# Recurrent layer: rates and scans of the first three chunks placed on either side of the sixth convolution; attention's norm broadcast issued one filling step earlier

## The chip, the cores and the metric

One NeuronCore of one Trainium2 chip runs the whole program. The metric is the time of one execution in device microseconds (us). A core has five engines that run side by side, each with its own queue, strictly in the order of that queue: TensorE (PE, matrix products into PSUM banks, with its weight loads PEld), VectorE (DVE), ScalarE (ACT), GpSimd (POOL) and SyncE (SP, which here only issues DMAs). Engines meet through semaphores: an instruction starts when its queue has reached it and what it waits for is done.

## The reference

Two layers of an encoder over 512 positions of width 1024, in float32. The first layer mixes by stick-breaking attention, the second by a gated recurrence; each is followed by an MLP, and a norm ends it.

```python
for layer in range(DEPTH):                       # DEPTH = 2
    h = rms_norm(x, norm_mix[layer])
    y = stick_breaking_attention(h, ...) if layer % 2 == 0 else rglru_block(h, ...)
    x = x + y
    h = rms_norm(x, norm_mlp[layer])
    x = x + squared_relu_mlp(h, mlp_w1[layer], mlp_w2[layer])
return rms_norm(x, norm_final)

def rglru_block(h, ...):
    proj = h @ w_in
    gate = jax.nn.gelu(proj[..., :RG_WIDTH])
    xc = causal_depthwise_conv(proj[..., RG_WIDTH:], conv_w, conv_b)       # 4 taps
    r = sigmoid(blocks(xc) @ w_a + b_a);  i = sigmoid(blocks(xc) @ w_x + b_x)   # 16 blocks of 64
    log_a = -8.0 * r * softplus(-lam)
    a = exp(log_a);  mult = sqrt(-expm1(2.0 * log_a))
    hs = scan over positions of (a, mult * i * xc)       # h[t] = a[t] h[t-1] + b[t]
    return (hs * gate) @ w_o
```

In the attention, `z` is the score of a query and a key, scaled; the weight of a key is sigmoid(z) times the product of sigmoid(-z) over the keys between it and the query.

## The kernel before

Activations lie transposed, 128 features by 512 positions, as eight chunks numbered 0 to 7. A float32 product is made of three fast ones: each operand is split into a high half (a copy by ACT, `wh`, `bh`, `xgh`) and a low half (a subtraction by DVE, `wl`, `bl`, `xgl`), and TensorE adds high x high, high x low and low x high (lines 197 to 199). A dense product of one chunk is 24 such products of 128x512 from one slab of weights (512 KB), which SP loads into `raw`, ACT copies to `wh` (line 185) and DVE subtracts to `wl` (line 192). From the fourth convolution to the last gate the low half of a slab is instead made by POOL (line 188) and a DMA that adds (line 189).

TensorE's order is written out by hand. The other engines' queues are laid out by a planner, which goes by priorities and by `issue_after` edges ("not before that instruction in the queue"): the helper `after(...)` sets one.

**Attention, first 105 us.** TensorE is filled with steps of dense products (queries, keys, values), and scores and values are slipped between them by due times. The norm of the input is not yet known when the first queries and keys are made; `inverse()` supplies it in two steps: after filling step `SUMS` = 5 the sums of squares are turned into `rc` and a diagonal `diag`, and after filling step `BROAD` = 9 a product with `diag` (line 422) broadcasts it over partitions and ACT copies it to SBUF as `r` (line 425). For the first pair of heads each score `z` is multiplied by `r` on DVE (`keep`, line 536) before ACT's two sigmoids (lines 538, 539) and DVE's scan (line 549). Scores turn through two `z` banks, so the third score waits until the first has been read by line 536.

**Recurrence, about 595 to 705 us.** The program's order is the list of calls at the end of `with ExitStack() as rctx`: `conv`, `gates`, `gate`, `recur`, `gated`. For chunk c,

- `conv(c)`: a dense product; DVE scales it by the norm (line 1071); ACT begins the convolution (1078) and DVE adds three taps (1080); ACT and DVE split it into high half (1086) and low half (1087). Convolutions have the planner's high priority.
- `gates(c)`: six products (lines 1100 to 1102, three for each of two gates; 1100 needs the high half, 1102 the low half), two sigmoids (1107, 1108), and `i * xc` on DVE (1109).
- `recur(chunks)`: for each chunk tanh (1119) and exp (1121) on ACT, 1122 and 1124 on DVE, 1123 on POOL; then for each chunk a square root (1127), a product (1128) and the scan (1131) on DVE.
- `gate(c)`: a dense product, scaled by the norm (1137). `gated(chunks)`: gelu (1142), product with the scan (1144), split (1145, 1146).

ACT changes its function table when it passes between sigmoid or tanh, exp, square root and gelu; each change is an instruction of its own, ACT_TABLE_LOAD. The chunks go through `recur` as 0 to 2, 3 to 5, and 6 and 7. The first group's call stands ahead of `conv(5)`, the sixth convolution. TensorE's order there is: convolution 4, gates 3, convolution 5, gates 4, gate 3, convolution 6, gates 5, gate 4, convolution 7, gates 6, gate 5, gate 6, gates 7, gate 7, then the output products.

Of the kernel before, what the change touches and what calls it, by code (L numbers as in the profile page):

```python
# [13 lines left out]
AF = mybir.ActivationFunctionType  # L14
ALU = mybir.AluOpType
# [5 lines left out]
C = D // P  # L21
# [19 lines left out]
HOLD = 3  # L41
LESS = 4
SUMS = 5
BROAD = 9
EARLY = 5


# [1 line left out]
def hybrid_encoder(  # L49
# [22 lines left out]
    V, A, G, PE = nc.vector, nc.scalar, nc.gpsimd, nc.tensor  # L72
# [941 lines left out]
    with ExitStack() as rctx:  # L1014
# [25 lines left out]
        def after(act):  # L1040

            return tc.issue_after(act.ins) if act is not None else nullcontext()

        xc, aa, om, z, hs, gin, gw = ({} for _ in range(7))

        TURNS = ["acc", "acc", "t", "t", "o", *("acc", "acc", "t", "t") * 3]
        turns = [0, 0]
# [44 lines left out]
        def gates(c):  # L1092
            nonlocal sig
            xch, xcl = gin[c]
            gh, gl = gw[c]
            pg = []
            for i in range(2):
                pi = bank("zzoo"[turns[1] % 4])
                turns[1] += 1
                PE.matmul(pi, gh[:, i, :], xch, start=True, stop=False)  # L1100
                PE.matmul(pi, gl[:, i, :], xch, start=False, stop=False)
                PE.matmul(pi, gh[:, i, :], xcl, start=False, stop=True)
                pg.append(pi)
            if c + 3 < C:
                gw[c + 3] = gate_weights(c + 3)
            with after(mark), after(begin):
                A.activation(aa[c], pg[0], AF.Sigmoid, bias=col("b_a")[:, c : c + 1])
                sig = A.activation(om[c], pg[1], AF.Sigmoid, bias=col("b_x")[:, c : c + 1])
            V.tensor_tensor(xc[c], om[c], xc[c], ALU.mult)

        def recur(chunks):
            nonlocal mark

            for c in chunks:
                a0 = rp2.tile([P, S], F32, tag="a0", name="a0")
                d = rp2.tile([P, S], F32, tag="d", name="d")

                with after(sig), after(high if c == 1 else None):
                    ex = A.activation(om[c], aa[c], AF.Tanh, scale=c4[:, c : c + 1])
                with after(ex):  # L1120
                    ex = A.activation(a0, aa[c], AF.Exp, scale=c8[:, c : c + 1])
                V.scalar_tensor_tensor(d, a0, 1.0, om[c], ALU.add, ALU.mult)
                G.tensor_scalar(aa[c], d, -1.0, 1.0, ALU.mult, ALU.add)
                V.scalar_tensor_tensor(xc[c], a0, 1.0, xc[c], ALU.add, ALU.mult)
            for c in chunks:
                with after(ex):
                    mark = A.activation(om[c], om[c], AF.Sqrt)
                V.tensor_tensor(xc[c], xc[c], om[c], ALU.mult)

                with after(tap if c < 6 else None):  # L1130
                    V.tensor_tensor_scan(om[c], aa[c], xc[c], 0.0, ALU.mult, ALU.add)
                hs[c] = om[c]

# [14 lines left out]
        sig = begin = tap = high = low = None  # L1148
        for what, c in (
            (conv, 0), (conv, 1), (conv, 2), (gate, 0), (gate, 1), (gates, 0), (conv, 3), (gates, 1),  # L1150
            (gate, 2), (gates, 2), (conv, 4), (gates, 3), (recur, range(3)), (conv, 5), (gates, 4),
            (gate, 3), (conv, 6), (gates, 5), (gate, 4), (conv, 7), (recur, range(3, 6)), (gates, 6),
            (gate, 5), (gated, range(6)), (gate, 6), (gates, 7), (recur, range(6, C)), (gate, 7),
            (gated, range(6, C)),
        ):
            with tc.high_priority() if what is conv else nullcontext():
                what(c)
# [166 lines left out]
```

## Time and profile before

| what | value |
|---|---|
| median of 3 runs | 1074.24 us (1074.09 to 1075.43) |
| the profiled execution's own time | 1074.38 us |
| its span, first to last instruction | 1072.4 us |
| TensorE busy | 1058.7 us, 99% |
| DVE / ACT / POOL busy | 821.3 / 568.6 / 170.8 us |
| granted TensorE clock | 0.998 |

The profiled execution takes 1.98 us more than its span and stands 0.14 us above the median. In the rows that follow, a timeline row gives start, duration, engine, line, operation, output and input, and in square brackets the idle time of the engine before it with what ended that time. A row of waits gives the total, the number of waits and the longest. "Busy" for TensorE is partly modelled, so short gaps between products are not seen as idle time.

### The profile page before, as it was taken

To read this page: it belongs to the slowest core of one execution; us is meant where nothing else is said; L and a number is where in the kernel's file an instruction comes from. 1 tells how busy PE (TensorE), PEld (TensorE's weight loads), DVE (VectorE), ACT (ScalarE), POOL (GpSimd) and SP (SyncE) were. 2 spreads that over 40 slices of the span, in tenths; PEclk is the share of its full clock that TensorE was granted. 3 is DMA by queue.
4 is the path that set the end of the run, shared out by engine and by line. 5 is a ranking of instruction groups with operands and counts; after the bars stand their busy time and mean duration, and the time that the engine had idled before them with its cause. 6 is when DMAs were issued, how large, how long until landed. Compare 5 with 4: busy or idle time off the path is not lost.

```text
span 1072.4 us, 13604 instructions
## 1 busy us (share of the span) xinstructions
PE 1058.7 (99%) x4992; PEld 878.4 (82%) x4992; DVE 821.3 (77%) x1073; ACT 568.6 (53%) x826; POOL 170.8 (16%) x199
## 2 busy tenths in 40 slices
PE   9999999999999999999999999999999999999997
PEld 7888888888888888888888877887888888888885
DVE  7788787839896697596688869975786597597777
ACT  6777676726554444344345477944454344344345
POOL 2344443410000000000001655122000000000003
PEclk9999999999999999999999999999999999999999
DMA  7745454517215206305342694243205305305103
GB/s 237 198 118 145 128 146 107 171 53 255 79 40 182 93 20 179 116 15 183 99 85 72 167 215 130 82 174 101 95 24 192 99 20 177 118 13 184 60 12 107
DMA packets 44034, 125.71 MB, mean 117 GB/s; under 512 B 7744, under 2 KB 8512, under 8 KB 43968
## 3 DMA queue, kind: packets, MB, share of 16 engines
q1 hardware_dynamic: 41088, 115.94, 34.7%
q0 software_dynamic: 2304, 8.39, 4.5%
q8 instruction: 39, 0.64, 0.3%
q10 hardware_dynamic: 576, 0.52, 0.2%
q14 instruction: 27, 0.22, 0.1%
HBM read 104.91 MB, written 2.10 MB: 100 GB/s over the span
## 4 chain that ended last, share of the span: by engine, by line
PE 88%; DVE 6%; ACT 3%; DMA 1%; issue 1%; SPq 0%; ACTq 0%; DVEq 0%
PE ps_t L874 9%; PE ps_acc L199 6%; PE ps_acc L197 6%; PE ps_acc L198 6%; PE ps_o L874 6%; PE ps_z L874 6%; PE ps_acc L874 4%; PE ps_o L197 4%; PE ps_o L198 4%; PE ps_o L199 4%; PE ps_t L198 4%; PE ps_t L197 3%; PE ps_t L199 3%; PE ps_z L198 3%; PE ps_z L197 3%; PE ps_z L199 3%
## 5 line engine op out<-in xcount | busy, mean ns | idle before, releaser
L185 ACT CAST wh<-raw 128x1024 fp32r<-128x1024 f32 (+2 forms) x136 | 119.7, 900 | 129.8 <-PE ps_o L199 33.6
L840 ACT CAST wh<-b 128x1024 fp32r<-128x1024 f32 x96 | 100.3, 1051 | 132.0 <-PE ps_o L874 25.0
L192 DVE TENSOR_TENSOR wl<-raw,wh 128x1024 fp32r<-128x1024 f32 (+2 forms) x126 | 131.0, 1056 | 23.3 <-ACT wh L185 23.1
L841 DVE TENSOR_TENSOR wl<-b,wh 128x1024 fp32r<-128x1024 f32 x96 | 118.4, 1236 | 23.9 <-ACT wh L840 23.8
L197 PE MATMUL ps_acc<-xgh,wh 128*128 128x512 f32 x304 | 122.5, 403 | 0.4 <-ACT wh L166 0.4
L199 PE MATMUL ps_acc<-xgl,wh 128*128 128x512 f32 x304 | 119.1, 392 | 0.1
L198 PE MATMUL ps_acc<-xgh,wl 128*128 128x512 f32 x304 | 119.0, 392 | 0.1
L855 POOL DMA_DIRECT2D b<-in_w_dn x6 | 5.4, 905 | 637.8 <-DVE wl L841 314.9
L549 DVE TENSOR_TENSOR_SCAN scan<-keep,later 128x128 f32<-128x128 f32 (+1 forms) x64 | 58.1, 911 | 17.4 <-ACT keep L539 10.6
L197 PE MATMUL ps_o<-xgh,wh 128*128 128x512 f32 x176 | 69.5, 395 | 0.2 <-DVE x L701 0.2
L198 PE MATMUL ps_o<-xgh,wl 128*128 128x512 f32 x176 | 68.6, 390 | 0.0
L199 PE MATMUL ps_o<-xgl,wh 128*128 128x512 f32 x176 | 68.6, 390 | 0.0
L199 PEld LDWEIGHTS ps_acc<-xgl,wh 128*128 128x128 f32 x304 | 57.1, 188 | 12.7 <-DVE xgl L117 0.5
L794 ACT ACTIVATE u<-u 128x512 f32<-128x512 f32 x64 | 39.3, 630 | 52.1 <-DVE u L793 52.1
L197 PE MATMUL ps_t<-xgh,wh 128*128 128x512 f32 x168 | 66.5, 396 | 0.0
L197 PEld LDWEIGHTS ps_acc<-xgh,wh 128*128 128x128 f32 x304 | 57.3, 188 | 10.6 <-ACT wh L166 0.7
L198 PE MATMUL ps_t<-xgh,wl 128*128 128x512 f32 x168 | 65.7, 391 | 0.0
L198 PEld LDWEIGHTS ps_acc<-xgh,wl 128*128 128x128 f32 x304 | 57.3, 188 | 10.1 <-DVE wl L167 0.8
L199 PE MATMUL ps_t<-xgl,wh 128*128 128x512 f32 x168 | 65.5, 390 | 0.0
L553 POOL TENSOR_TENSOR w<-w,scan 128x128 f32<-128x128 f32 (+1 forms) x64 | 51.9, 813 | 53.6 <-DVE scan L549 50.8
L862 DVE TENSOR_TENSOR b<-b,b 128x1024 f32<-128x1024 f32 x46 | 55.9, 1217 | 0.2
L804 DVE TENSOR_TENSOR u<-u 128x256 f32<-128x256 f32 x128 | 49.4, 419 | 2.4 <-ACT u L794 1.7
(325 smaller groups left out, 2749.1 us busy)
## 6 DMA issues: line engine op xcount, KB each, us to landing
raw<-in_w_m SPq DMA_DIRECT2D x64, 512.0 KB, 3.6
b<-in_w_dn SPq DMA_DIRECT2D x48, 512.0 KB, 4.2
raw<-in_w_dn SPq DMA_DIRECT2D x16, 512.0 KB, 3.5
raw<-in_w_in SPq DMA_DIRECT2D x16, 512.0 KB, 4.2
raw<-in_w_qk SPq DMA_DIRECT2D x12, 512.0 KB, 3.6
wl<-raw POOLq DMA_DIRECT2D x10, 512.0 KB, 6.2
x<-in_xT SPq DMA_DIRECT2D x16, 256.0 KB, 4.2
raw<-in_w_ro SPq DMA_DIRECT2D x8, 512.0 KB, 4.2
```

Source lines behind the costliest of these rows:

```text
L185: A.copy(wh[:, k, :], raw[:, k, :])
L192: V.tensor_tensor(wl[:, k, :], raw[:, k, :], f(wh[:, k, :]), ALU.subtract)
L197: PE.matmul(ps, wh, ah, start=start, stop=False)
L198: PE.matmul(ps, wl, ah, start=False, stop=False)
L199: PE.matmul(ps, wh, al, start=False, stop=stop)
L549: V.tensor_tensor_scan(sc[:, S - n : S][:, ::-1], keep[:, :n][:, ::-1], later[:, S - n :][:, ::-1], 1.0, ALU.mult, ALU.max,)
L553: G.tensor_tensor(wt, wt, sc[:, S - n + 1 : S + 1], ALU.mult)
L804: V.tensor_tensor(u[:, out, :], u[:, x, :], u[:, y, :], op)
L840: A.copy(wh, raw)
L841: self.cut = V.tensor_tensor(wl, raw, f(wh), ALU.subtract)
L862: self.sum = V.tensor_tensor(raw, raw, self.raws[to, g], ALU.add)
L874: PE.matmul(ps, x[:, block, ts], y[:, jj, cols], start=first and n == 0, stop=last and n == 2, skip_group_check=not new,)
```

## The change

Two things are changed.

First, `recur` is cut in two. `rates(chunks)` is its first half, tanh, exp and the three element operations; the new `recur(chunks)` is its second half, square root, product and scan. For the first group `rates` stays ahead of `conv(5)`, and `recur` is called behind it, with new edges: square roots not ahead of ACT's begin of convolution 5, products and scans not ahead of the low half of convolution 5 (`low`). For the other groups the two are called one behind the other. In the first group the edge to a high half (`high`) moves from the tanh of chunk 1 to the exp of chunk 0, so all three tanh go ahead of the split of convolution 4, and its exp behind it. In `gates`, `i * xc` (line 1109, now 1110) gets an edge behind the latest low half.

Second, `BROAD` goes from 9 to 8.

```diff
-BROAD = 9
+BROAD = 8
...
-            V.tensor_tensor(xc[c], om[c], xc[c], ALU.mult)
-
-        def recur(chunks):
-            nonlocal mark
+            with after(low):
+                V.tensor_tensor(xc[c], om[c], xc[c], ALU.mult)
+
+        def rates(chunks):
 
             for c in chunks:
                 a0 = rp2.tile([P, S], F32, tag="a0", name="a0")
                 d = rp2.tile([P, S], F32, tag="d", name="d")
-
-                with after(sig), after(high if c == 1 else None):
+                with after(sig):
                     ex = A.activation(om[c], aa[c], AF.Tanh, scale=c4[:, c : c + 1])
-                with after(ex):
+
+                with after(ex), after(high if c == 0 else None):
                     ex = A.activation(a0, aa[c], AF.Exp, scale=c8[:, c : c + 1])
...
+            exps[chunks[-1]] = ex
+
+        def recur(chunks):
+            nonlocal mark
             for c in chunks:
-                with after(ex):
+
+
+                with after(exps[chunks[-1]]), after(begin if c < 3 else None):
                     mark = A.activation(om[c], om[c], AF.Sqrt)
-                V.tensor_tensor(xc[c], xc[c], om[c], ALU.mult)
-
-                with after(tap if c < 6 else None):
+                with after(low if c < 3 else None):
+                    V.tensor_tensor(xc[c], xc[c], om[c], ALU.mult)
+                with after(low if c < 3 else tap if c < 6 else None):
                     V.tensor_tensor_scan(om[c], aa[c], xc[c], 0.0, ALU.mult, ALU.add)
...
-            (gate, 2), (gates, 2), (conv, 4), (gates, 3), (recur, range(3)), (conv, 5), (gates, 4),
-            (gate, 3), (conv, 6), (gates, 5), (gate, 4), (conv, 7), (recur, range(3, 6)), (gates, 6),
-            (gate, 5), (gated, range(6)), (gate, 6), (gates, 7), (recur, range(6, C)), (gate, 7),
+            (gate, 2), (gates, 2), (conv, 4), (gates, 3), (rates, range(3)), (conv, 5),
+            (recur, range(3)), (gates, 4),
+            (gate, 3), (conv, 6), (gates, 5), (gate, 4), (conv, 7), (rates, range(3, 6)), (recur, range(3, 6)), (gates, 6),
+            (gate, 5), (gated, range(6)), (gate, 6), (gates, 7), (rates, range(6, C)), (recur, range(6, C)), (gate, 7),
```

No instruction's shape or count changes and no arithmetic does. TensorE's order stays, but for the broadcast product, which goes ahead of one step (three products). On the other engines the order can be listed from the built programs without running them. In the recurrence, behind the edges named above: on DVE the three products 1128 and the three scans 1131 of the first group, which lay between the taps of convolution 5, stand together behind its low half and ahead of line 1071 of convolution 6; further on, the scaled gate 5 (1137) and the subtraction of a `w_ro` slab (192) stand ahead of the low half of convolution 7, not behind it; on ACT the split of convolution 6 stands ahead of the third tanh of the second group. In the attention: ACT's copy of `r` goes ahead of the split of the second pair's queries (line 312), DVE's first `keep` (536) stands behind two subtractions of line 192 that followed it, and ahead of the low half of those queries (313); a later slab of `w_qk` is loaded ahead of four copies of queries on SP's queue, copied by ACT between the first sigmoids, and subtracted by DVE around the third `keep`, where all three came later before.

More of the change, by code (lines that the diff above doesn't have):

```diff
@@ L1042, in after @@
             return tc.issue_after(act.ins) if act is not None else nullcontext()
-        xc, aa, om, z, hs, gin, gw = ({} for _ in range(7))
+        xc, aa, om, z, hs, gin, gw, exps = ({} for _ in range(8))
         TURNS = ["acc", "acc", "t", "t", "o", *("acc", "acc", "t", "t") * 3]
```

## The prediction

> **What bounds the kernel now.** I read the page first (its head and its first part), then TensorE's waits, then the timeline of each engine around the longest of them.
>
> ```profile
> span 1072.4 us, 13604 instructions
> PE 1058.7 (99%) x4992; PEld 878.4 (82%) x4992; DVE 821.3 (77%) x1073; ACT 568.6 (53%) x826; POOL 170.8 (16%) x199
> ```
>
> ```profile
> PE ps_o L1100 <- ACT bh L1086: 2.1, 1, 2.1
> PE ps_z L530 <- DVE keep L536: 1.2, 1, 1.2
> ...
> PE ps_z L1102 <- DVE bl L1087: 0.9, 2, 0.5
> ```
>
> TensorE is the bound: 13.7 us of the span are idle, most of it at the two ends. So time is won or lost only where TensorE waits, and the two longest waits inside are the two that the change stands beside. The most it can win is what these places cost, read from TensorE's timeline:
>
> ```profile
> 32.49 0.28 PE L448 MATMUL ps_acc<-wh,xgl 128*128 128x256 f32 x1
> 33.95 0.44 PE L530 MATMUL ps_z<-kh,q 128*128 128x384 f32 x1 [1.18 <-DVE keep L536]
> ...
> 640.54 0.39 PE L199 MATMUL ps_t<-xgl,wh 128*128 128x512 f32 x1
> 643.15 0.40 PE L1102 MATMUL ps_z<-bl,gh 128*128 128x512 f32 x1
> ...
> 654.22 0.39 PE L199 MATMUL ps_acc<-xgl,wh 128*128 128x512 f32 x1
> 656.68 0.50 PE L1100 MATMUL ps_o<-bh,gh 128*128 128x512 f32 x1 [2.07 <-ACT bh L1086]
> 658.21 0.39 PE L1102 MATMUL ps_o<-bl,gh 128*128 128x512 f32 x1
> 669.98 0.39 PE L1102 MATMUL ps_z<-bl,gh 128*128 128x512 f32 x1
> 682.30 0.39 PE L1102 MATMUL ps_o<-bl,gh 128*128 128x512 f32 x1
> ```
>
> Unhindered, 128x512 products start 0.23 us apart (rows of conv 4 and 5 stages; 0.23 x 6 = 1.4 for the six of a `gates`). Gates 4 should end with a start at 640.54 + 1.4 = 641.94 and do at 643.15: 1.2 lost. Gates 5: 655.6 against 658.21: 2.6 lost. With 0.2 of gates 2, the recurrence can give 4.0. The third score, due at 32.61, starts at 33.95: 1.34. Gates 6 and 7 (669.98 and 682.30 are their first products with a low half) wait for nothing now.
>
> **The attention part (`BROAD`).**
>
> ```profile
> 29.66 0.59 ACT L312 CAST xh<-ps_t 128x512 fp32r<-128x512 f32 x1 [4.63 <-DMA q<-xl]
> 30.14 0.59 ACT L425 COPY r<-ps_z 128x512 f32<-128x512 f32 x1
> ```
>
> ```profile
> 33.61 0.28 DVE L536 TENSOR_TENSOR keep<-ps_z,r 128x128 f32<-128x128 f32 x1
> ```
>
> ACT sits 4.63 us at line 312 until a DMA has read the buffer that it overwrites, and the copy of `r`, whose product was made long before, is queued behind it. Changed, the broadcast product goes one step (three products, 0.7 us) earlier, and `r` is queued ahead of line 312. Then `r`, two halves of a `w_v` slab and two of a `w_qk` slab are copied in the idle 4.63 us, DVE has four subtractions behind them (each 0.6, to 30.3), and the first `keep` ends near 30.6, not at 33.89. The third score finds its bank free at 32.61: **1.34 won**. Line 312 itself still starts at 29.66, so the second pair's queries are no sooner.
>
> Next behind it is the fifth score, now at 38.45, then due at 37.1, which waits for the third `keep`. Ahead of that `keep` DVE now has a subtraction of the next `w_qk` slab, whose copy blocks ACT until its load has landed. SP issues that load earlier, where its queue comes free of `kl`:
>
> ```profile
> 29.18 1.84 SPq L331 DMA_DIRECT2D kl<-tl  x2
> 34.34 0.58 SPq L179 DMA_DIRECT2D raw<-in_w_qk  x1
> ```
>
> ```profile
> DMA to landing us min/median/max: 3.8/3.8/3.8
> ...
> DMA to landing us min/median/max: 5.1/6.1/7.1
> ```
>
> The first row is this load at 34.34, the second the two `w_v` loads issued right behind it. Issued at 31.05 and landing L later, half a copy (0.62), half a subtraction (0.6), two hand-overs and the `keep` (0.54 for 128x384) follow: the `keep` ends at 32.9 + L. With L up to 4.2 the fifth score is in time; each microsecond more costs one. The bounds are 3.8 (nothing lost) and 7.1 (2.9 lost). I take 4.5, near the same load's own row, since four copies of `kl` and `kh` are still under way: 0.3 lost. The four query copies behind it on SP's queue are late by about 1 us; they serve scores of the second pair near 50 us, and cost nothing. Gain here: **1.05** (1.34 down to -1.6). The rest of attention is full TensorE time, and ACT and DVE there wait for scores, so the gain is carried on.
>
> **The recurrence: the waits removed.**
>
> ```profile
> 634.13 1.05 ACT L185 CAST wh<-raw 128x1024 fp32r<-128x1024 f32 x1 [3.05 <-PE ps_t L199]
> 637.21 0.72 ACT L1119 ACTIVATE om<-aa,c 128x512 f32<-128x512 f32 x1
> ...
> 640.47 0.60 ACT L1086 CAST bh<-bt 128x512 fp32r<-128x512 f32 x1
> ...
> 650.31 1.04 ACT L185 CAST wh<-raw 128x1024 fp32r<-128x1024 f32 x1
> 656.01 0.62 ACT L1086 CAST bh<-bt 128x512 fp32r<-128x512 f32 x1 [4.66 <-DVE bt L1080]
> 658.00 0.78 ACT L1078 ACTIVATE bt<-ps_acc,colt 128x512 f32<-128x512 f32 x1 [0.41 <-DVE ps_acc L1071]
> ...
> 661.84 0.72 ACT L1121 ACTIVATE a<-aa,c 128x512 f32<-128x512 f32 x1
> ```
>
> Changed, the high half of chunk 4 follows three tanh (0.63 each) on ACT, at 637.2 + 1.9 = 639.1 and not 640.47; its low half is done by 640.5, gates 4 (due 640.77, low 641.2) don't wait: 1.2 won. Between 634.13 and 651.35 ACT is never idle and does the same list of work in both orders (no table load more or less), so the high half of chunk 5 can start at 651.3 (651.1 with the 0.2 of gates 2). It started at 656.01 because DVE's last tap was behind two scans; with the scans behind the low half, the taps are done by 649, even with the third one held behind the scaled gate 3 (TensorE's end, 647.7). Low half of chunk 5 at 651.7 to 652.4; gates 5, due near 653 by then, don't wait: 2.6 won.
>
> **The recurrence: what is late next.** The scans don't vanish. Behind that low half DVE has three products, 1109 of chunk 4 and three scans, and only then line 1071 of convolution 6.
>
> ```profile
> 647.52 1.22 DVE L1131 TENSOR_TENSOR_SCAN om<-aa,bt 128x512 f32<-128x512 f32 x1
> 651.52 2.05 DVE L1131 TENSOR_TENSOR_SCAN om<-aa,bt 128x512 f32<-128x512 f32 x1
> 657.27 0.69 DVE L1071 TENSOR_TENSOR ps_acc<-ps_acc,r 128x512 f32<-128x512 f32 x1
> 665.07 0.68 DVE L1124 SCALAR_TENSOR_TENSOR bt<-a,bt 128x512 f32<-128x512 f32 x1
> 665.67 0.68 DVE L1137 TENSOR_TENSOR z<-ps_t,r 128x512 f32<-128x512 f32 x1
> 672.75 1.52 DVE L1080 SCALAR_TENSOR_TENSOR bt<-ps_t,colt,bt 128x511 f32<-128x511 f32 x2
> 676.41 3.44 DVE L1131 TENSOR_TENSOR_SCAN om<-aa,bt 128x512 f32<-128x512 f32 x3
> 679.77 0.66 DVE L1087 TENSOR_TENSOR bl<-bt,bh 128x512 fp32r<-128x512 f32 x1
> 683.97 1.21 DVE L192 TENSOR_TENSOR wl<-raw,wh 128x1024 fp32r<-128x1024 f32 x1
> ...
> 701.87 1.29 DVE L1146 TENSOR_TENSOR bl<-z,bh 128x512 fp32r<-128x512 f32 x2
> ```
>
> ```profile
> 645.89 3.07 POOL L188 TENSOR_SCALAR wl<-wh 128x1024 fp32r<-128x1024 f32 x1 [1.30 <-ACT wh L185]
> ...
> 651.45 2.78 POOL L188 TENSOR_SCALAR wl<-wh 128x1024 fp32r<-128x1024 f32 x1 [0.79 <-ACT wh L185]
> ```
>
> Operations of 512 follow each other every 0.60 (665.07 to 665.67), scans every 1.13 (3.44 for three), taps every 0.76, a subtraction of a slab takes 1.14 to the next start. Line 1071 of chunk 6: 651.7 + 0.6 (low half) + 4 x 0.6 + 3 x 1.13 = 658.1. To that comes what POOL costs DVE: the scan at 651.52 took 2.05, 0.84 more than the others, when POOL's line 188 had just begun; that of 647.52, inside another such line, lost nothing. Line 188 now begins near 651.2, beside the low half of chunk 5. Bounds 0 and 0.84, I take 0.4: 658.5, against 657.27 now, though TensorE has by then finished convolution 6 at 653.2 (654.61 less 1.4).
>
> From there as now: 0.73 to ACT's 1078 and 4.56 to the end of the exp of chunk 3 (658.00 to 662.56), then 1122, 1124, a scaled gate, 1122, 1124 at 0.6 each, and the low half of chunk 6, started at 658.5 + 5.3 + 3.0 = 666.8, done at 667.5. TensorE needs it 11.77 after the end of gates 5 (658.21 to 669.98): 658.21 - 4.0 + 11.77 = 666.0. **A new wait of 1.6 at gates 6.**
>
> Behind that low half: 1109 of chunk 5 (0.6), done 0.1 later, the third tanh (0.63), its exp (0.76) and hand-over: 2.7 to the third 1122. Then DVE has 1122, 1124 and 1071 of chunk 7 (1.8), three products (1.8), two slab subtractions (2.3, one behind the cast, 0.3), three taps (2.2), three scans (3.4), the scaled gate 5 (0.6): 12.4 to the low half of chunk 7: 666.8 + 2.7 + 12.4 = 681.9, done at 682.6, product at 682.7. Now it is at 682.30, with 679.77 for the low half: the scaled gate and the slab, 1.74, stood behind it. TensorE would be ready at 667.5 + 12.32 = 679.9: **a new wait of 2.8 at gates 7.** New waits 1.6 + 2.8 = 4.4 against 4.0 removed: the recurrence **loses 0.4** (0 without POOL's share, 0.85 with all of it). Whatever TensorE wins before, gates 7 start when DVE's queue lets them.
>
> The Trainium skill's page "SBUF — State Buffer", section "Who interferes with whom", speaks against the change: a DVE operation with two SBUF inputs and a GpSimd operation that reads SBUF exclude each other, and the loser blocks for the whole instruction. By that rule the low half of chunk 5 would wait until line 188 ends; the scan of 647.52, two SBUF inputs inside line 188, disagrees here.
>
> Behind gates 7 nothing changes: the last low half of the gated chunks is done at 703.2 today, and the output products reach it some 5 us later. The first group's `1123` of chunks 1 and 2 stand behind a line 188 (2.8) on POOL, done near 648, and scans need them from 655: nothing. The gate weights' copies move by one load on SP and are read microseconds later: nothing.
>
> **Sum.** 1074.38 - 1.05 + 0.4 = 1073.73 for the profiled execution, which stood 0.14 above the median: **1073.6**. A measurement of this kernel tells about 0.2%, 2.15 us, from no change.
>
> **Rivals.**
>
> *Slower: the early slab lands late.* If the load behind the `kl` copies takes 7.1, as the second `w_v` load did, the attention loses 1.6 in place of winning 1.05: 1073.6 + 2.65 = 1076.3. From 5.6 on the attention gains nothing. For it: DMAs are already under way. Against: the same load took 3.8 at its place of today.
>
> *POOL holds DVE for a whole line.* Line 188 from 651.2 to 654.0 holds the low half of chunk 5 back by 2.3, not 0.4, and the whole chain with it: 1075.5. For it: 2.05 at 651.52. Against: 1.22 at 647.52.
>
> *The waits stay away.* If DVE's chain from chunk 5 to 7 ran far enough ahead of the sum, 4.0 and 1.05 would both be kept: 1069.2. It would need line 1071 of chunk 6 by 657 and the scaled gate and slab of 1.74 out of the way of gates 7; the queue's order speaks against it. Half of it gives 1071.5.
>
> *The attention's gain is lost on the way* (DVE nearly full from 35 to 60 us): 1074.6, no change.
>
> **Chances.** Forecast 0.5 (1072.8 to 1074.4); gain lost on the way 0.15; waits stay away, wholly or half, 0.15; POOL holds DVE 0.1; late slab 0.1. Faster by over 0.2% (under 1072.1): the third case and little of the first, 0.18. Slower by over 0.2% (over 1076.4): half of the late slab, or both slow cases together, 0.1. Within: 0.72. The range reaches into the cases on both sides, 1071.3 to 1075.7.
>
> **What would show it.** `r` copied before 28 us, no wait of TensorE at line 530 over 0.3; no wait at gates 4 and 5; new waits for `bl` at gates 6 (about 1.6) and gates 7 (about 2.8); line 1071 of chunk 6 between 658 and 659 in today's time less 1.05. A wait at gates 7 under 1.5, or a wait at the fifth score over 1, makes the prediction wrong.

## The result, and the profile after

| | before | after |
|---|---|---|
| median | 1074.7 us (17 runs, 1073.87 to 1077.09) | 1077.36 us (17 runs, 1076.13 to 1080.73) |
| ratio after to before | | 1.002 (95% interval 1.0013 to 1.0028) |
| the profiled execution | 1074.38 us, span 1072.4 | 1080.73 us, span 1079.0 |

The forecast was 1073.6, within a range of 1071.3 to 1075.7. The change makes the kernel about 2 us slower, 0.2%, at the edge of what a measurement tells. The profiled execution of after is the slowest of its 17, 3.4 us above the median; what it shows has to be held against other executions, which the experiments supply.

The head and the first part of the page of after:

```profile
span 1079.0 us, 13603 instructions
PE 1060.8 (98%) x4992; PEld 880.6 (82%) x4992; DVE 821.9 (76%) x1073; ACT 567.7 (53%) x826; POOL 168.9 (16%) x199
```

TensorE's waits in after (for what, us in total, number, longest):

```profile
PE ps_z L530 <- DVE keep L536: 3.1, 1, 3.1
PE ps_o L1102 <- DVE bl L1087: 2.6, 1, 2.6
PE ps_z L1102 <- DVE bl L1087: 2.0, 2, 1.7
```

The 2.1 us at gates 5 (line 1100) are gone, and two others stand at the top. TensorE's timeline in after, at the places that the prediction quoted of before (the third score, the seventh score, the last product of gates 4 and of gates 5, the waiting product of gates 6 and of gates 7):

```profile
32.46 0.33 PE L530 MATMUL ps_z<-kh,q 128*128 128x384 f32 x1
...
44.21 0.45 PE L530 MATMUL ps_z<-kh,q 128*128 128x384 f32 x1 [3.11 <-DVE keep L536]
...
645.84 0.39 PE L1102 MATMUL ps_z<-bl,gh 128*128 128x512 f32 x1
658.32 0.39 PE L1102 MATMUL ps_o<-bl,gh 128*128 128x512 f32 x1
672.07 0.50 PE L1102 MATMUL ps_z<-bl,gh 128*128 128x512 f32 x1 [1.67 <-DVE bl L1087]
687.29 0.68 PE L1102 MATMUL ps_o<-bl,gh 128*128 128x512 f32 x1 [2.61 <-DVE bl L1087]
```

TensorE's products come in nearly the same order in all kernels of this case, so the start of one product in two timelines can be subtracted. The table gives by how much TensorE is behind the profiled execution of before (us, positive is later); the columns are times in before. The kernels e1 to e11 are the experiments below.

| kernel | 32 | 36 | 50 | 255 | 267 | 640 | 662 | 680 | 705 |
|---|---|---|---|---|---|---|---|---|---|
| after | -0.14 | -1.60 | 3.35 | 3.16 | 4.15 | 3.89 | 0.13 | 2.22 | 6.66 |
| e1, recurrence alone | 0.16 | -0.90 | -0.16 | 0.05 | 0.74 | 0.52 | -3.24 | -1.17 | 3.29 |
| e2, broadcast alone | -0.12 | -1.57 | 2.36 | 2.32 | 2.30 | 2.28 | 2.33 | 2.34 | 2.34 |
| e11, after once more | 0.64 | -0.81 | 1.89 | 2.31 | 3.45 | 3.39 | -0.37 | 1.68 | 6.08 |
| e9, with repairs | 0.12 | -1.14 | -0.43 | -0.43 | 0.17 | -0.13 | -3.89 | -3.45 | -1.38 |

From 705 us to the end nothing moves by more than 0.05. In after, the third score gains 1.5 and what follows the seventh gives back 5.0 by 50 us. The recurrence gains 3.8 between 640 and 662, as forecast; gates 6 give back 2.1 and gates 7 then 4.4. But the waits are 3.11, 1.67 and 2.61. At the first and the last of them about 1.8 us more went than TensorE waited. (About 0.2 of it come with the wait itself: across the 2.61 at gates 7 the shift jumps from 2.22 to 4.99.)

**Where the 1.8 us are.** Behind both waits TensorE works at half speed. The windows view of after (window, its length, then busy time and instruction count of PE, PEld, DVE, ACT and POOL, then the granted TensorE clock, the DMA share and GB/s); the windows are cut where the clock changes:

```profile
42.33:45.74 3.41, 1.53 (x12) 1.53 (x13) 3.41 (x6) 2.23 (x5) 2.75 (x3) 1.00 0.93 224
45.74:49.15 3.41, 3.41 (x17) 3.22 (x16) 2.58 (x5) 1.81 (x4) 2.92 (x6) 0.50 0.51 115
49.15:52.56 3.41, 3.41 (x21) 3.00 (x21) 3.19 (x5) 3.41 (x8) 1.29 (x2) 1.00 0.00 0
...
684.04:687.45 3.41, 0.80 (x4) 0.35 (x3) 3.41 (x5) 3.41 (x7) 0.00 (x0) 1.00 0.00 0
687.45:690.86 3.41, 3.41 (x9) 2.64 (x10) 3.41 (x7) 3.38 (x5) 0.00 (x0) 0.50 0.42 154
690.86:694.27 3.41, 3.41 (x16) 2.77 (x15) 3.41 (x5) 3.38 (x5) 0.00 (x0) 1.00 0.20 48
```

A granted clock of 0.50 holds for exactly 3.41 us each time; 9 products fit where the next window has 16. Half of 3.41 is 1.71 us lost. And the clock does not fall at the wait's end: the seventh score starts at 44.21, and TensorE runs at full clock until 45.74. The two starts of half clock lie 687.45 - 45.74 = 641.71 apart, 188.0 times 3.413. So the clock looks at windows of 3.413 us on a fixed raster, a grid of such windows laid end to end through the whole run. The one from 42.33 was idle for 3.41 - 1.53 = 1.88, the one from 684.04 for 2.61. In before, the wait of 2.07 at gates 5 ended at 656.68 (its records have the clock full from 6.65 on, and 190 windows later one begins at 655.18), and its windows read:

```profile
651.77:655.18 3.41, 2.84 (x13) 2.02 (x11) 3.41 (x3) 0.00 (x0) 3.00 (x2) 1.00 0.61 115
655.18:658.59 3.41, 1.91 (x7) 1.30 (x8) 2.67 (x5) 2.16 (x3) 0.35 (x1) 1.00 1.00 246
```

The raster cut that wait in two, 0.57 and 1.50 us idle, and no half clock followed. The Trainium skill's page "TensorE: Matmul & The Clock Gate", section "What's actually happening", says that the clock is gated by a window of 4096 cycles, 3413 ns, that runs freely and does not start with the kernel. The traces agree: 3.41 us, and the raster begins elsewhere in each execution. Its section "Why this matters for your kernels" asks for no idle gap over some 3 us; here 1.88 us within one window was enough.

**Where the 3.11 us are.** Three views of after: ACT's split of the second pair's keys, DVE's split with the `keep` behind it, and from the view of line 304 the time from issue to landing of the four query copies:

```profile
40.68 0.62 ACT L312 CAST xh<-ks 128x512 fp32r<-128x512 f32 x1 [3.41 <-DMA q<-xh]
```

```profile
42.03 0.69 DVE L313 TENSOR_TENSOR xl<-ks,xh 128x512 fp32r<-128x512 f32 x1 [3.63 <-DMA q<-xl]
...
43.88 0.28 DVE L536 TENSOR_TENSOR keep<-ps_z,r 128x128 f32<-128x128 f32 x1
```

```profile
DMA to landing us min/median/max: 7.7/7.9/8.0
```

The same row of before:

```profile
DMA to landing us min/median/max: 2.2/2.3/2.6
```

The queries and the keys of a pair are split through the same two buffers, `xh` and `xl`. In before SP issued the copies that read them ahead of two slab loads, and they landed 2.3 us later; in after they stand behind the loads and land 7.9 us after their issue. The split of the keys waits for them on ACT and DVE, and the `keep` that frees the seventh score's bank is queued behind it on DVE.

### The profile page after: what moved, and what is told of

It is laid out like the page before. It is cut to its first block, busy times and chain, and to the rows that moved or that the text cites. A ratio compares the mean times of both kernels' runs of the same rounds, so it can differ in the third digit from the quotient of the medians.

```text
span 1079.0 us, 13603 instructions
## 1 busy us (share of the span) xinstructions
PE 1060.8 (98%) x4992; PEld 880.6 (82%) x4992; DVE 821.9 (76%) x1073; ACT 567.7 (53%) x826; POOL 168.9 (16%) x199
## 4 chain that ended last, share of the span: by engine, by line
PE 84%; DVE 7%; ACT 4%; DMA 3%; issue 2%; SPq 1%; DVEq 0%; ACTq 0%
PE ps_t L874 9%; PE ps_o L874 6%; PE ps_acc L199 6%; PE ps_acc L198 6%; PE ps_acc L197 6%; PE ps_z L874 6%; PE ps_acc L874 4%; PE ps_o L197 4%; PE ps_o L199 4%; PE ps_o L198 4%; PE ps_t L197 3%; PE ps_t L198 3%; PE ps_t L199 3%; PE ps_z L198 3%; PE ps_z L197 3%; PE ps_z L199 3%
```

## The experiments

Each kernel was run beside the first kernel ("before") on the same chip, in three sets on three chips; before's median was 1076.06 us for e1 to e4 (35 runs), 1076.31 for e5 to e8 (33) and 1076.5 for e9 to e11 (18), higher than the 1074.7 of the 17 runs above, so ratios to before in the same set are what is compared. "Recurrence" in the following is the shift from 267 to 705 us.

**e1: the recurrence alone.** The changed kernel with

```diff
-BROAD = 8
+BROAD = 9
```

> The changed recurrence with the broadcast at its old step (9). Theory A (the recurrence is where the time went): the waits taken away (0.24 + 0.39 + 0.75 + 2.3 = 3.7 us in the changed kernel's trace) are outweighed by those put in their place (gates 6 1.7, gates 7 2.6) and by TensorE running at half clock for 3.41 us behind the longest of them, which costs another 1.7; the kernel is 1 to 2.7 us slower than before, and its trace shows a wait of about 2.6 us at line 1102. Rival B (the attention is where it went, and the recurrence comes out as forecast): within 0.6 us of before. Rival C (the half clock has nothing to do with the waits): slower by about 0.7 us alone, with no stretch at half clock in the trace.

Measured: 1076.91 us (12 runs), ratio 1.001 (1.0001 to 1.002). In its trace the waits are 1.67 and 2.62, the window from 680.69 to 684.10 is 2.63 idle, the next one is at half clock, and the recurrence costs 3.29 - 0.74 = 2.55, as in after (2.51). Theory A holds in the trace: 0.9 us of waits and 1.7 of clock. In time the recurrence costs less, 1.1 us by the ratio (0.1 to 2.2), near the lower edge of theory A: the trace is compared with one execution of before that had no half clock, the ratio with all of its runs, most of which have one (see e8). A second thing is in e1: with before's own order in the attention, the third score does not wait. DVE's rows ahead of the first `keep` in before, and in e1:

```profile
31.80 0.69 DVE L313 TENSOR_TENSOR xl<-ps_t,xh 128x512 fp32r<-128x512 f32 x1 [5.34 <-ACT wh L166]
```

```profile
30.86 0.69 DVE L313 TENSOR_TENSOR xl<-ps_t,xh 128x512 fp32r<-128x512 f32 x1 [4.31 <-ACT xh L312]
...
32.72 0.29 DVE L536 TENSOR_TENSOR keep<-ps_z,r 128x128 f32<-128x128 f32 x1
```

Both rows name a releaser that was already done. What line 313 waits for is the copy to `q` (line 331) that still reads `xl`: in before it was issued at 27.26 and landed at 31.26, in e1 it was issued at 27.98 and landed at 30.32, and in both line 313 starts 0.54 us behind the landing. In the seven traces with this order it starts 0.52 to 0.54 us behind it. So a transfer that took 4.0 us, and 2.3 to 3.5 in the other six, made the first `keep` of before's profiled execution late: it starts at 33.61, in e1 at 32.72. The other traces with that order (e3, e5, e6, e8, e9) have no wait of more than 0.5 at these scores either.

**e2: the broadcast alone.** The kernel before with `BROAD = 8`.

> The kernel before with the broadcast one step sooner (BROAD = 8) and nothing else. Theory A: the wait of the third score (1.34 us) is gone, but the query copies of the second pair, issued behind slab loads, land some 8 us after their issue, the split of the second keys waits for them, and the seventh score waits 2 to 3 us in place of 1.24; where that wait fills more than half of one of TensorE's clock windows of 3.41 us, another 1.7 us go. Together between 1 us faster and 2 us slower than before, run by run. Rival B (the early load costs little, as forecast): 1.0 us faster in every run, a seventh wait under 1.6 us.

Measured: 1076.55 us (11 runs, 1073.54 to 1078.70), ratio 1.0003 (0.9994 to 1.0012). In its trace the copies land after 6.3 to 6.8 us (about 8 expected), the seventh score waits 1.89 (2 to 3 expected), and the windows view shows

```profile
40.28:43.70 3.42, 1.53 (x12) 1.33 (x11) 2.77 (x5) 2.28 (x6) 1.28 (x3) 1.00 1.00 280
43.70:47.11 3.41, 3.41 (x16) 3.22 (x15) 3.41 (x6) 1.55 (x4) 3.28 (x5) 0.50 0.86 216
```

1.89 idle, then half clock. The 2.1 us wait of gates 5, cut by the raster into pieces of which the larger was 1.20 idle, made none. Over its runs the broadcast is worth nothing that can be measured, and rival B's 1.0 us in every run is not there. Theory A describes what happened, with both of its sizes a little too high.

**e3: the recurrence kept warm.** As e1, with in `gates`

```diff
-                PE.matmul(pi, gh[:, i, :], xch, start=True, stop=False)
+                [PE.matmul(pi, gh[:, i, :], gin[6][0], start=True, stop=True) for _ in range(5 * (c == 7 and i == 0))]; PE.matmul(pi, gh[:, i, :], xch, start=True, stop=False)
```

> As the recurrence alone, with five more products of 512 columns in front of the products of gates 7; they read the sixth chunk's finished half, write a bank that the first real product then overwrites, and add nothing to the output. They lie in the time in which TensorE waits for the low half of the seventh convolution. Theory A (the half clock comes of the wait): the wait shrinks from 2.6 to about 1.4 us, the low half lands when it did, no stretch at half clock follows, and the kernel is 1.3 us (1.7 us in about three of four executions) faster than the recurrence alone. Rival (the products behind the wait are slow for another reason, their operands or the traffic): the stretch at half rate stays, and the time is the same as of the recurrence alone or longer by up to 1.1 us.

Measured: 1076.39 us (11 runs, 1075.41 to 1077.08), ratio 1.0005 (0.9997 to 1.0014). The windows around gates 6 and gates 7:

```profile
666.42:669.83 3.41, 1.74 (x7) 1.14 (x7) 3.41 (x6) 1.26 (x2) 0.99 (x1) 1.00 0.00 0
669.83:673.24 3.41, 3.41 (x9) 2.64 (x8) 3.01 (x5) 3.38 (x6) 1.00 (x1) 0.50 0.43 150
...
683.48:686.90 3.42, 3.42 (x15) 2.56 (x14) 3.42 (x7) 3.12 (x5) 0.00 (x0) 1.00 0.47 153
686.90:690.31 3.41, 3.41 (x16) 2.75 (x15) 3.41 (x6) 3.39 (x6) 0.00 (x0) 1.00 0.00 0
```

Behind gates 7 TensorE is now always busy and the clock stays full: the same products of line 197 that ran at half rate in e1 run at full rate, so it was neither their operands nor the traffic (a DMA share of 0.49 in e1's slow window, 0.47 here). In this execution the clock fell behind gates 6 instead, whose 1.67 us lay wholly in one window. That made gates 7 wait less, so the trace does not give the 1.3 us by itself; the median is 0.5 us under e1's, less than the 1.3 of theory A, and the runs from 1078 us up, three of e1's twelve, are gone. The mechanism is shown, its mean price only in direction.

**e4: the keys' halves in buffers of their own.** As e2, with

```diff
-            xh = hp.tile([P, S], F32R, tag=f"{tag}h", name=f"{tag}h", bufs=1)
-            xl = hp.tile([P, S], F32R, tag=f"{tag}l", name=f"{tag}l", bufs=1)
+            xh = hp.tile([P, S], F32R, tag=f"{tag}h", name=f"{tag}h", bufs=1 + 2 * (tag == "t"))
+            xl = hp.tile([P, S], F32R, tag=f"{tag}l", name=f"{tag}l", bufs=1 + 2 * (tag == "t"))
...
-            h, l = parted(ks, "x")
+            h, l = parted(ks, "t" if pair == 1 else "x")
```

> The kernel before with BROAD = 8, and the halves of the second pair's keys in buffers of their own (tags th and tl, three buffers each) in place of the pair of buffers that the second pair's queries hold until their copies have landed. Theory A (the copies' landing is what holds the seventh score): the split of the keys no longer waits for a DMA, the seventh score's wait goes back to 1.2 us or less, no half clock, and the third score's 1.34 us is kept: 1.0 to 2.5 us faster than before. Rival (the seventh score is held by what stands before it on VectorE and ScalarE anyway): as the broadcast alone.

Measured: 1075.82 us (11 runs), ratio 0.9998 (0.9989 to 1.0007). The seventh score no longer waits (the sixth waits 0.45, as in e1), and on DVE's timeline in e4 the keys' split is no longer held by a DMA:

```profile
38.03 0.69 DVE L549 TENSOR_TENSOR_SCAN scan<-keep,later 128x256 f32<-128x256 f32 x1
38.63 0.72 DVE L313 TENSOR_TENSOR tl<-ks,th 128x512 fp32r<-128x512 f32 x1
```

So the shared buffers and the late copies were what held the seventh score. But 1.0 to 2.5 us of gain did not come: against the six traces of the old order in which the third score hardly waits, the sooner broadcast has little to win. The order at gates 5 is before's, and here the wait there lies in one window, 2.06 idle. So the trace also shows what before can lose (windows view of e4):

```profile
654.29:657.70 3.41, 1.35 (x7) 0.76 (x5) 2.67 (x4) 1.06 (x2) 1.46 (x2) 1.00 0.52 126
657.70:661.11 3.41, 3.41 (x9) 2.49 (x8) 2.92 (x5) 2.82 (x5) 0.00 (x0) 0.50 0.96 199
```

**e5: the low half of convolution 7 ahead of the scans.** As e1, with

```diff
-                with after(low if c < 3 else tap if c < 6 else None):
+                with after(low if c < 6 else None):
                     V.tensor_tensor_scan(om[c], aa[c], xc[c], 0.0, ALU.mult, ALU.add)
```

> The changed recurrence alone (broadcast at step 9), with the scans of chunks 3 to 5 behind the low half of the seventh convolution in place of its last tap, so that VectorE makes that half before 3.4 us of scans. Theory A (the scans and what stands with them ahead of the low half make the wait of gates 7, and that wait makes the half clock): the wait of 2.6 us is gone, no half clock near 687, 2.6 to 4.3 us faster than the recurrence alone and 1 to 3 us faster than before; the wait of 1.7 at gates 6 stays, and some executions lose 1.7 us to half clock behind it. Rival (the late scans are waited for next, at the gated products): the gain is given back, time within 0.5 us of the recurrence alone.

Measured: 1075.36 us (11 runs), ratio 0.9994 (0.9985 to 1.0002). DVE in e5:

```profile
679.97 0.68 DVE L1087 TENSOR_TENSOR bl<-bt,bh 128x512 fp32r<-128x512 f32 x1
680.57 3.45 DVE L1137 TENSOR_TENSOR_SCAN om<-aa,bt 128x512 f32<-128x512 f32 x3
```

Gates 7 wait for nothing. The recurrence costs 0.97 - 0.41 = 0.56, with one half window behind gates 6 in it (the window from 666.18 to 669.60 is 1.68 idle). Theory A in the mechanism; of the gain over e1, 2.0 us in the traces and 1.7 by the two ratios came, less than its 2.6. Against before it is 0.6 us faster by the ratio, an interval that includes no change, and not the 1 to 3 us of theory A.

**e6: both low halves first.** As e5, with the two operations of chunk 4's rates (lines 1122, 1124) behind convolution 6's low half:

```diff
-            low = V.tensor_tensor(xcl, x0, f(xch), ALU.subtract)
+            low = lows[c] = V.tensor_tensor(xcl, x0, f(xch), ALU.subtract)
...
-                V.scalar_tensor_tensor(d, a0, 1.0, om[c], ALU.add, ALU.mult)
+                with after(lows[6] if c == 4 else None): V.scalar_tensor_tensor(d, a0, 1.0, om[c], ALU.add, ALU.mult)
...
-                V.scalar_tensor_tensor(xc[c], a0, 1.0, xc[c], ALU.add, ALU.mult)
+                with after(lows[6] if c == 4 else None): V.scalar_tensor_tensor(xc[c], a0, 1.0, xc[c], ALU.add, ALU.mult)
```

> As the kernel before this one, and the rates of chunk 4 (two VectorE operations of 0.68 us) behind the low half of the sixth convolution. Theory A: the wait of gates 6 shrinks from 1.7 to 0.5 us or less, no window of TensorE's clock is more than half idle in the recurrence, and no half clock is seen between 600 and 700 us: 1.2 to 2 us faster than the kernel before this one, 2.5 to 4.5 us faster than the first kernel. Rival (two products by the square root now stand ahead of the seventh convolution's scaling on VectorE): up to 2 us come back as a wait at gates 7.

Measured: 1074.69 us (11 runs), ratio 0.9985 (0.9976 to 0.9994). The waits of gates 6 and 7 are under 0.6, but the wait moved on, to the first output product that needs a gated low half. TensorE, then DVE, in e6:

```profile
689.82 0.79 PE L199 MATMUL ps_o<-bl,wh 128*128 128x512 f32 x1 [1.99 <-DVE bl L1152]
```

```profile
684.34 3.69 DVE L1150 TENSOR_TENSOR z<-om,z 128x512 f32<-128x512 f32 x6
687.96 1.21 DVE L192 TENSOR_TENSOR wl<-raw,wh 128x1024 fp32r<-128x1024 f32 x1
689.09 0.68 DVE L1152 TENSOR_TENSOR bl<-z,bh 128x512 fp32r<-128x512 f32 x1
```

All 1.99 lie in one window, and half clock follows from 689.86. Neither theory had named this place: "no half clock is seen between 600 and 700 us" failed, and the kernel is 1.6 us faster than before, not 2.5 to 4.5. DVE has no idle time here, so its order decides which product is late.

**e7: e6 with e4's attention.**

> As the kernel before this one, with the broadcast at step 8 and the halves of the second pair's keys in buffers of their own. Theory A: the attention's sooner broadcast is worth nothing or up to 1 us where its loads don't hold the scores: the same time as the kernel before this one to 1 us less, 2.5 to 5 us faster than the first kernel. Rival (the sooner loads crowd the transfers of the first scores): up to 1 us slower than the kernel before this one.

Measured: 1074.35 us (11 runs, 1072.16 to 1077.18), ratio 0.9985 (0.9973 to 0.9998): as e6, with the same wait of 2.0 and half clock from 689.90. That is theory A's "same time"; the gain of at most 1 us can't be told from none. The 2.5 to 5 us against the first kernel did not come (1.6).

**e8: before, kept warm at gates 5.** The kernel before with four more products in front of gates 5:

```diff
-                PE.matmul(pi, gh[:, i, :], xch, start=True, stop=False)
+                [PE.matmul(pi, gh[:, i, :], gin[c - 1][0], start=True, stop=True) for _ in range(4 * (c == 5 and i == 0))]; PE.matmul(pi, gh[:, i, :], xch, start=True, stop=False)
```

> The kernel before, with four more products of 512 columns (0.9 us) in front of gates 5, where TensorE waits 2.07 us for a high half; they read the fourth chunk's half, write a bank that the first real product overwrites, and add nothing to the output. Theory of the clock windows (a window of 3.41 us that is more than half idle makes the next one run at half clock, and where the windows lie differs from execution to execution): the kernel before loses 1.7 us at this wait in about six of ten executions, so that the median falls by about 1 us and the slow ones of its runs thin out, while its fastest time stays. Rival (the half clock needs a wait of 2.6 us or more, and the kernel before never loses it): no change, or up to 0.5 us slower for the other order of the work behind it.

Measured: 1076.60 us (11 runs, 1075.38 to 1076.96), ratio 1.0002 (0.9993 to 1.0011). The wait shrank to 1.10 and no half clock follows it:

```profile
656.45 0.50 PE L1100 MATMUL ps_o<-bh,gh 128*128 128x512 f32 x1 [1.10 <-ACT bh L1086]
...
689.68 0.50 PE L197 MATMUL ps_o<-bh,wh 128*128 128x512 f32 x1 [0.90 <-ACT aa L1107]
```

The median did not fall, and the fastest time rose by 1.4. The planner laid the work behind the extra products out in another order, and a wait of 0.90 at 689.68 and 0.3 more came of it (1.2 later between 680 and 692 us). Its runs stay within 1.6 us where before's 33 reach from 1073.96 to 1078.89, 8 of them above 1077: its runs have lost both ends. The mean granted clock, on record for every run, says why. One stretch of 3.41 us at half clock takes 0.0016 from it. Of before's 86 runs in the three sets, 61 have a mean of 0.997 or less, with a median time of 1076.61 us; 25 have 0.998 or more, with a median of 1074.89, 1.7 us less. Of e8's 11 runs none is under 0.998. So before loses half a window in about 7 of 10 runs, and the filled wait ends that; the 1.2 us of the other order then take the gain back (0.7 x 1.7 = 1.2). A mean near 0.998 alone does not decide (before's trace has it without a half window, e3's with one), and it does not say where in a run the half window lies; e4's trace shows one behind gates 5.

**e9: the first two gated chunks first.** As e6, with

```diff
-            with after(mark), after(begin):
+            with after(mark), after(firsts[0] if c == 7 else begin):
...
-                with after(low):
+                with after(firsts[1] if 1 < c < 6 else low):
                     V.tensor_tensor(z[c], hs[c], z[c], ALU.mult)
-                A.copy(bh[:, c, :], z[c])
-                V.tensor_tensor(bl[:, c, :], z[c], f(bh[:, c, :]), ALU.subtract)
+                hi = A.copy(bh[:, c, :], z[c])
+                lo = V.tensor_tensor(bl[:, c, :], z[c], f(bh[:, c, :]), ALU.subtract)
+                firsts = (hi, lo) if c == 1 else firsts
```

> The kernel with both low halves first (broadcast at step 9), and of the six gated products the first two, with their high and low halves, ahead of the other four on VectorE and ahead of gates 7's sigmoids on ScalarE. Theory A (what remains there is one wait of 2.0 us for the first gated low half, and the half clock behind it): that wait falls to 0.6 us or less, no window between 640 and 710 us is half idle, no half clock there, 1.5 to 3.5 us faster than with both low halves first in their median, 3 to 5 us faster than the first kernel. Rival (VectorE is simply full in this stage, and the wait moves on to the next half that is made later): waits of together 1.5 us or more at lines 197 to 199 between 688 and 710 us, and no gain.

Measured: 1073.46 us (6 runs, 1072.68 to 1074.30), ratio 0.9972 (0.9961 to 0.9983), 3.0 us faster than before. What is left of waits from 640 to 712 us on TensorE:

```profile
679.50 0.50 PE L1102 MATMUL ps_o<-bl,gh 128*128 128x512 f32 x1 [0.50 <-DVE bl L1087]
687.31 0.50 PE L197 MATMUL ps_o<-bh,wh 128*128 128x512 f32 x1 [1.01 <-ACT aa L1107]
```

No half clock before the program's end, and no run of the six has a mean clock under 0.998. Against e6 the gain is 1.4 us by the two ratios, at the lower edge of theory A. The recurrence gains 1.55, against 2.55 lost in e1. The 1.01 is new: the bank of the output product is still read by gates 7's sigmoids, which now stand behind two more copies on ACT.

**e10: e9 with e4's attention.**

> As the kernel before this one, with the broadcast at step 8 and own buffers for the second pair's key halves. Theory A: within 1 us of the kernel before this one on either side, since the third score's wait that the sooner broadcast was to remove (1.2 us in the profiled execution of the first kernel) is not there in other executions of the same queue order. Rival (the wait is the rule and that removal a gain): 1.0 us or more faster than the kernel before this one.

Measured: 1072.35 us (5 runs, 1072.08 to 1073.95), ratio 0.9962 (0.9949 to 0.9975), against e9's 0.9972; the intervals overlap, so theory A's "within 1 us" stands (0.001 of 1076 is 1.1 us) and a small gain isn't excluded. By its median it is the fastest kernel of this case.

**e11: the changed kernel once more.**

> The changed kernel as it is, beside the others on one chip. Theory A: 1 to 3 us slower than before in the median, with a wait of about 2.6 us at gates 7 in its profile in any case; the seventh score's wait (3.1 us in its first profile) comes out differently, between 0.5 and 3 us, and a half clock follows each wait that fills more than half (1.7 us) of one of TensorE's windows of 3.41 us, and no other. Rival (the clock follows the length of the wait alone, from 2.6 us on): the half clock at 687 us and, if the seventh wait is again under 2.6 us, none near 45 us.

Measured: 1078.34 us (12 runs, 1075.01 to 1080.81), ratio 1.0017 (1.0006 to 1.0028), as the first time. The seventh score waits 1.17 in this execution, not 3.11:

```profile
41.54:44.95 3.41, 2.24 (x18) 2.04 (x17) 2.92 (x5) 2.92 (x7) 1.77 (x3) 1.00 0.81 219
44.95:48.36 3.41, 3.41 (x29) 3.32 (x28) 3.38 (x6) 1.32 (x4) 3.29 (x5) 1.00 0.65 150
```

No half clock there; at gates 7 it is as in after (2.51 idle in a window, half clock from 686.66). The attention costs 1.7 all the same (0.64 to 2.31 between 32 and 255 us), in a wait of 0.81, this 1.17 and smaller ones. The 0.81 are the fifth score's: here the early `w_qk` slab landed 5.45 us after its issue, in after 4.60. The rival's threshold of 2.6 us is refuted by e2, e3 and e4, not by this run.

**The windows of all traces together.** For each window between 30 and 700 us with 1 us idle or more (its length less PE's busy time, same view as above):

| idle in the window | windows | next window |
|---|---|---|
| 1.88 to 2.63 | after (1.88, 2.61), e1 2.63, e2 1.89, e4 2.06, e6 1.99, e7 2.01, e11 2.51 | half clock, 8 of 8 |
| 1.67 to 1.68 | e3, e5 / after, e1, e11 | half clock in 2, full in 3 |
| 1.00 to 1.50 | before 1.50 and 1.18, after 1.22, e2 1.20, e11 1.17, e8 1.10, e10 1.04 and 1.00, e9 1.01 | full, 9 of 9 |

The line lies between 1.5 and 1.9 us, about half a window (1.7), and is not sharp in this view, in which the end of each product is modelled. The two ends of a run fit less well: in e10 half clock followed a window with 1.29 idle at 4.86 us, and in e9 a window with 1.86 idle at 1063.02, where the last products end, was followed by full clock.

## Why the prediction was wrong

The forecast was a gain of 0.65 us, from 1.05 won in the attention and 0.4 lost in the recurrence. The change lost 2.2 us by the ratio (1.4 to 3.0; 1.8 in e11). Taken alone, the broadcast lost 0.3 (e2) and the recurrence 1.1 (e1), each to about 1 us, so the two terms add up to the whole within their intervals.

- **The recurrence's waits: right, nearly to the row.** DVE in after:

```profile
662.60 0.67 DVE L1071 TENSOR_TENSOR ps_acc<-ps_acc,r 128x512 f32<-128x512 f32 x1
...
670.92 1.10 DVE L1087 TENSOR_TENSOR bl<-bt,bh 128x512 fp32r<-128x512 f32 x1
...
681.47 3.45 DVE L1137 TENSOR_TENSOR_SCAN om<-aa,bt 128x512 f32<-128x512 f32 x3
684.83 0.67 DVE L1143 TENSOR_TENSOR z<-ps_acc,r 128x512 f32<-128x512 f32 x1
685.41 1.22 DVE L192 TENSOR_TENSOR wl<-raw,wh 128x1024 fp32r<-128x1024 f32 x1
686.54 0.69 DVE L1087 TENSOR_TENSOR bl<-bt,bh 128x512 fp32r<-128x512 f32 x1
```

  Less the 4.15 us by which this execution was late at 267 us, line 1071 of chunk 6 is at 658.45 (forecast 658.5), the low half of chunk 6 done at 667.87 (667.5), that of chunk 7 at 683.08 (682.6). Removed: 3.8 between 640 and 662 us, forecast 4.0. New waits: 1.67 and 2.61, forecast 1.6 and 2.8.
- **The step that failed there** is the sum "New waits 1.6 + 2.8 = 4.4 against 4.0 removed: the recurrence loses 0.4". It prices a wait at its length and puts the clock at nothing. The wait at gates 7 lay whole or nearly whole in one clock window in all three traces of this order (after, e1, e11) and cost about 1.7 us more, so the recurrence loses 2.5 against the profiled execution of before. Against before's runs as a whole it loses 1.1 (e1: 0.1 to 2.2), because most of those lose half a window themselves (61 of 86, see e8); so the missing term stood on both sides of the sum, and the 0.4 would lie inside that interval. By the raster, a wait of 2.61 escapes only where both its parts are under 1.7, that is in (2 x 1.7 - 2.61) / 3.41 = 23 of 100 executions; before's 2.07 escapes in 39 of 100 (both are estimates, from the windows table, with the line at 1.7, and a raster that may lie anywhere; the mean clocks of before give 25 of 86). The profiled execution of before was one that escaped, and nothing in its rows said that it could have been otherwise.
- **The attention failed at** "The four query copies behind it on SP's queue are late by about 1 us; they serve scores of the second pair near 50 us, and cost nothing." They do serve those scores. They also free the two buffers through which the second pair's keys are split, and they land 6 us later, not 1 (7.9 us after issue, not 2.3). The slab itself stayed within its bounds (4.60 us in after, 4.5 taken; 5.45 in e11, where the fifth score waited 0.81). In after the fifth score did not wait. Instead of the gain of 1.05 the broadcast alone gave 0.3 us more time (e2: 0.6 less to 1.3 more).
- **"1.34 won" at the third score** came in after (32.46 in place of 33.95), but it was credited to the copy of `r` alone. In before's profiled execution the first `keep` was also late by the landing of a copy; in six other traces with the same order the score hardly waits. So the gain was an accident of that execution, and the broadcast is worth nothing that can be measured (e2: 1.0003; e4: 0.9998, each to 0.0009).
- **"which stood 0.14 above the median"**: of three runs. In sets of 18 to 35 runs before's median is 1076.06 to 1076.5. The profiled execution had no half clock, and none of the 0.2 to 1.3 us that all other traces but e2's lose at the norm behind the attention (255 to 267 us in the table). That loss is seen with either broadcast and either recurrence, where a slab of the MLP lands late (ACT waits 4.28 us for it in after, 2.98 in before, 3.29 in e2); why it stays away in before and e2 is open.
- **The rivals.** "The early slab lands late" gave 1076.3, by a transfer that comes late in the attention; the place was right and the transfer another. "The attention's gain is lost on the way" came true in its outcome, through the seventh score's wait and not through a full DVE. "The waits stay away" was ruled out by DVE's queue, rightly: it took e5, e6 and e9 to bring it about, by moving low halves ahead of scans and gated products. As to POOL, its line 188 and the low half of chunk 5 did meet; POOL, then DVE, in after:

```profile
655.33 2.77 POOL L188 TENSOR_SCALAR wl<-wh 128x1024 fp32r<-128x1024 f32 x1 [2.49 <-ACT wh L185]
```

```profile
655.78 1.12 DVE L1087 TENSOR_TENSOR bl<-bt,bh 128x512 fp32r<-128x512 f32 x1 [1.58 <-ACT bh L1086]
```

  The low half, 0.66 to 0.69 where POOL is idle, took 1.12 in the middle of line 188: 0.46 lost, the forecast's 0.4, and not the 2.3 of the rival "POOL holds DVE". The rule of the Trainium skill's page "SBUF — State Buffer", section "Who interferes with whom", that the loser blocks for the whole instruction, disagrees with these rows too.

## What to carry to other kernels

Price a wait of the engine that bounds the kernel by the clock window it may fill, not by its length alone: here a wait of 1.0 cost 1.3 (e9), one of 2.6 cost 4.4 in each of the three traces that had it. When a transfer is moved ahead of others on a queue, ask for each one it passes which buffer its landing frees and who writes that buffer next. Before a wait is booked as a gain, look whether a second execution of the same order has it; a wait that ends with a DMA's landing may not be there. And compare the new kernel with before's runs as a whole, since the profiled execution may have escaped a loss that most of them have.

## What the runs showed of the hardware

- TensorE's granted clock falls to half for exactly 3.41 us behind a window of a 3.413 us raster in which it was idle for more than about half (between 30 and 700 us: 8 of 8 from 1.88 us on, 2 of 5 at 1.67, 0 of 9 up to 1.50; the ends of a run fit less well), and the raster lies differently in each execution. The price is 1.7 us where TensorE is otherwise busy, and the slow stretch begins up to one window after the wait (1.5 us behind it in after).
- Four copies of 128 KB each that land 2.3 us after their issue ahead of two slab loads of 512 KB land 5.7 to 8.0 us after it when they are issued right behind these (six traces; 2.2 to 2.8 in the seven of the old order).
- The runs of before spread by 3.2 to 4.9 us in its four sets and those of the changed kernel by 4.6 and 5.8; those of e8 and e9, where no wait comes near the line, by 1.6.
